# Attention in a hybrid decoder layer: outputs computed transposed with the values as weights, queries and keys stored as high and low parts, and one hand-written order through attention and mix

## The chip, the cores and the metric

The kernel runs on one core of a Trainium2 chip. The metric is the device time of one execution in microseconds (us). The engines are TensorE (PE, with its weight loads PEld), VectorE (DVE), ScalarE (ACT), GpSimd (POOL) and SyncE (SP), which here only issues transfers. ACT and POOL can issue transfers too, each on a queue of its own.

## What is computed

One layer on x of 1024 tokens by 1024 channels, all in float32, with an attention group and a recurrence group side by side:

```python
h = _rms_norm(x, norm_mix_pre)
z = h @ w_in                                  # attention q, k, v (8 heads x 64); RWKV r, k, v, lora
attn = _rms_norm(_dilated_attention(q, k, v), attn_out_gain)
rw = _rwkv7(r, k, v, xw, xa, xg, ...)
x = x + _rms_norm(concatenate([attn, rw]) @ w_out, norm_mix_post)
h = _rms_norm(x, norm_ffn_pre)
f = square(relu(h @ w_ffn_up)) @ w_ffn_down
x = x + _rms_norm(f, norm_ffn_post)
```

The attention has three branches of (window, dilation), (128, 1), (512, 4) and (2048, 16), combined by their softmax denominators. The kernel computes them as one: a strip of additive terms that depend only on the distance of query and key says in how many branches a key counts, and one exponential with the row's extreme as its bias gives numerators and denominators together.

## The kernel before

**Precision.** Most large products are made of three: a float32 matrix is split into a high part in fp32r and the remainder, and `mm3` adds high by high, low by high and high by low. Scores take two: the 128 rows of the weights hold the query's high part (64 channels) over its low part, and the moving matrices hold the key's high (`kh`) or low part (`kl`) twice. The product of exponentials and values is in plain float32, which the trace shows as two records per instruction.

**Stages.** (a) Up to about 446 us come the projections (`z_…`, slabs of 128 output columns, two halves of 512 tokens each) and the recurrence (units `ab`, `e`, `c`, `g`; outputs `O`, `E`, `Y`). The projections are the filling: they run where the recurrence waits. Queries, keys and values of attention (`aq`, `ak`, `av`, one slab per pair of heads) go transposed, as channels by tokens, to DRAM in `zs_d`. (b) Attention, four pairs of heads one after the other. (c) The mix `[A, R] @ W_out` by tiles of 128 tokens, in the order 0, 4, 1, 5, 2, 6, 3, 7, each as an r half (`mxr`) and an a half (`mxa`) that accumulate into `pm`, with a norm and the residual. (d) The feed-forward part, from about 740 us to the end, with products `X`, `Y`, `Z`, `dX`, `dY`, `dZ`; the change leaves it as it is.

**Attention before** is `attn_pair(p)`. SP loads q and k of each head twice, onto partitions 0–63 and 64–127. POOL makes the high parts (`qs` L844, `kh` in `gcopy` L122), DVE the low parts (`qs` L845, `kl` L854). PE transposes the values to `Vt` (keys by channels). For each tile of 128 queries and each head: PE makes scores `pS` in up to two banks, DVE adds the strip and keeps the row's minimum (L890), ACT takes the exponential and its row sum (L893), PE transposes each 128 x 128 block (`pT`, L900), and ACT (L902) or DVE (L904) copies it to `PT`. Then `av` multiplies: `PT` of one block is the weight, 128 columns, and the 64 columns of `Vt` move; a tile of `po` has queries on its partitions. After four query tiles DVE takes reciprocals (L910) and scales (L912), SP stores to `a_d` as tokens by channels (L914), and ACT and DVE sum squares for the norm (L917, L918).

**The entry to the mix.** `half_a` loads a tile of `a_d`, ACT scales it by the norm's factor `sa` (L978), PE transposes it (L964, `mxta`), ACT and DVE split it. So the whole a half waits for `sa`, which needs the last squares. The r halves of three tiles are computed ahead; the third is tied behind the last `po`.

**What sets the order.** The recurrence with its projections is ordered by hand: `drive` walks a list of jobs with their conditions, keeps an estimated time, uses delays from the table `WAIT`, takes a projection step wherever no job is due, and so writes down the order of PE and SP. Attention is not under it: its order comes from the scheduler with a priority (`PRI[3]`), and the projections of the last pair (`rest`) and the weights of the mix are handed to the same scheduler after the first pair. From the first a half on, PE's order is by hand again.

Of the kernel before, what the change touches and what calls it, by code (L numbers as in the profile page):

```python
# [17 lines left out]
P = 128  # L18
# [12 lines left out]
WAIT = {'mrg1.0': 26.0, 'mrg1.3': 4.0, 'mrg2.0': 15.5, 'mrg3.0': 19.5, 'vo3_1': 10.5, 'pre1.0': 9.5, 'e0': 14.5, 'mrg0.0': 29.5, 'vo0_1': 18.5, 'pre3.0': 7.0, 'ab0': 13, 'ab1': 5.0, 'norm3': 3, 'norm2': 3.5, 'vo1_0': 6, 'pre0.0': 6.5, 'vo0_0': 13.0, 'mrg1.2': 5.0, 'vo2_1': 9.5, 'pre2.0': 9.0, 'vo1_1': 6.5, 'vo2_0': 8.0, 'vo3_0': 12.0, 'mrg3.1': 3.5, 'e2': 1, 'c2.2': 1, 'pre1.3': 4, 'T4': 1, 'mrg3.3': 1, 'e4': 1.0, 'VU3': 5.5, 'c3.1': 4.0, 'c6.2': 1.5, 'EO1_1': 1, 'PE4': 5.0, 'e1.0': 2.5, 'e5': 2.5, 'pre2': 0, 'EO0_1': 2, 'e6.0': 0, 'VU7': 1.5, 'ab0.0': 1.5, 'T5': 1, 'e7': 6, 'VU1': 5, 'ab5.0': 4, 'e6': 1.0, 'c4.0': 1, 'EO4_0': 11.0, 'e5.0': 0, 'ab2.0': 2.5, 'c1.1': 2.0, 'e3': 1.5, 'EO5_1': 5, 'VU4': 7.5, 'c1.2': 1, 'ab4': 0, 'e7.0': 2.5, 'EO5_0': 2.5, 'c5.2': 1, 'c2.1': 2.5, 'T1': 5, 'ab3': 0, 'pre1': 0, 'pre2.1': 0, 'mrg2.2': 4, 'c0': 4, 'EO2_1': 3, 'e1': 0}  # L31
# [9 lines left out]
def hybrid_kernel(tc, x, par, cst, strip, win, wup_lora, gup, gnwb, grow, wout, wup, wdown, out, dbg=None):  # L41
# [12 lines left out]
    with (  # L54
# [45 lines left out]
        a_d = dp.tile([S, 512], F32, name="a_d")  # L100
# [6 lines left out]
        bk_d = dp.tile([8, P, 2, 4, P], F32, name="bk_d")  # L107
        v_d = dp.tile([S, 512], F32, name="v_d")
# [228 lines left out]
        def gate():  # L337
            for t in range(8):
# [3 lines left out]
                go = evp.tile([P, 512], F32, name=f"go{t}", tag="ev", bufs=3)  # L342
# [292 lines left out]
        def unit_g(n):  # L635
# [24 lines left out]
            yield 0.0, 11.0  # L660
            nc.sync.dma_start(r_d[ts, :], Y)
            yield 0.0, 0.0

        def v_out(p, hf):
# [8 lines left out]
            vt = evp.tile([P, 512], F32, name=f"vt{p}_{hf}", tag="ev", bufs=3)  # L673
            vc = evp.tile([P, 512], F32, name=f"vc{p}_{hf}", tag="ev", bufs=3)
# [8 lines left out]
        def proj_spill(nm, i, shift):  # L683
            last = [None]

            def ev(hf, pz):
                zt_ = evp.tile([P, 512], F32, name=f"ev_{nm}_{hf}", tag="ev" if i >= 8 else "kr", bufs=3 if i >= 8 else 8)
# [6 lines left out]
                if i < 8:  # L694
                    KR[i, hf] = zt_
                elif i < 12:
                    VZ[i - 8, hf] = zt_
                else:
                    A.dma_start(zs_d[i, :, hf * 512:hf * 512 + 512], zt_)
# [33 lines left out]
        def drive(todo, jobs):  # L733


            now, done, live = 0.0, {}, []
            pre = lambda x: x if isinstance(x, tuple) else (x, 0.0)
            z = slabs(todo, done)
            jobs = list(jobs)
            while jobs or live:  # L740
# [22 lines left out]
                else:  # L763
                    step = next(z, None)
                    if step is None:
# [5 lines left out]
            return z  # L771
# [19 lines left out]
        todo += [(f"{n}{p}", 12 + 4 * j + p, False, "C7" if p == 3 else None) for p in range(4) for j, n in ((0, "aq"), (1, "ak"), (2, "av"))]  # L791
# [25 lines left out]
        order = {j[0]: i for i, j in enumerate(jobs)}  # L817
        with tc.manual_schedule(engines={mybir.EngineType.PE, mybir.EngineType.SP}):
            rest = drive(todo, jobs)
# [3 lines left out]
        ev_ctx = tc.tile_pool(name="ev2", bufs=2)  # L823
        evp = ev_ctx.__enter__()
# [5 lines left out]
        sq4 = cp.tile([P, 4, 8], F32, name="sq4")  # L830
        sa = cp.tile([P, 5, 8], F32, name="sa")[:, 0:2]
        stripT = ap_.tile([P, S], F32, name="stripT", bufs=1)
        nc.sync.dma_start(stripT, strip)

        last_av = [None]

        def attn_pair(p):
            QS, KH, KL = [], [], []
            for h in range(2):
                qr = ap_.tile([P, S], F32, name=f"qr{p}_{h}", tag="raw")  # L840
                for d in range(2):
                    nc.sync.dma_start(qr[own[d]], zs_d[12 + p, h * 64:h * 64 + 64, :])
# [602 lines left out]
```

## Time and profile before

| | |
|---|---|
| median of 3 runs | 1365.77 us (1364.53 to 1368.21) |
| the profiled execution | 1361.23 us, of which the span 1359.4 |
| granted TensorE clock, mean over the span | 0.991 |
| PE busy | 1307.3 us, 96% |
| DVE busy | 914.7 us, 67% |
| ACT busy | 625.0 us, 46% |
| attention, first scores to last output | 469.3 to 637.5 us |
| DMA | 231.02 MB, mean 170 GB/s |

Busy time says when an engine had an instruction in it, not that the engine went at its peak. Matmuls overlap in the pipeline, so the mean length of a record is longer than the distance between the starts of two; it is the distance that sets the time of a group.

### The profile page before, as it was taken

The numbers are of one execution on the slowest core, as the hardware profiler recorded it, in microseconds if no ns is written. First come the engines' busy times: TensorE is split into PE (matmuls) and PEld (weight loads), VectorE is DVE, ScalarE is ACT, GpSimd is POOL, SyncE is SP. The second block draws the span as 40 slices with busy tenths as digits, with TensorE's granted clock in tenths as the row PEclk, the third lists the DMA queues.
The fourth block names the chain that finished last, engine by engine and source line by source line (L and its number), as shares of the span: only waits on it lengthen the run. The fifth ranks groups of instructions, "written<-read, shape, count | busy, mean of one in ns | idle before, by whom it ended". The sixth has DMA issues, their size and how long they took to land.

```text
span 1359.4 us, 22401 instructions
## 1 busy us (share of the span) xinstructions
PE 1307.3 (96%) x8784; PEld 1086.4 (80%) x8784; DVE 914.7 (67%) x1647; ACT 625.0 (46%) x1026; POOL 44.7 (3%) x56
## 2 busy tenths in 40 slices
PE   6999999999999999999998999999999999999997
PEld 5777887788777798988887888888887888888885
DVE  7867658531678567655788986677766786445686
ACT  7652324233555367654656444343434344443442
POOL 0000000000000100110000000000000002000110
PEclk9999999899999999999999999999999999999999
DMA  7346746676685656321434344444366995346564
GB/s 255 114 170 163 194 125 179 184 206 204 182 248 145 194 145 181 102 55 38 138 121 139 132 168 152 168 153 150 132 209 217 322 349 172 95 139 200 186 215 157
DMA packets 161193, 231.02 MB, mean 170 GB/s; under 512 B 51680, under 2 KB 88800, under 8 KB 161088
## 3 DMA queue, kind: packets, MB, share of 16 engines
q1 hardware_dynamic: 153024, 208.62, 48.8%
q10 hardware_dynamic: 8064, 20.98, 4.6%
q8 instruction: 69, 1.13, 0.4%
q14 instruction: 36, 0.29, 0.1%
HBM read 156.66 MB, written 72.89 MB: 169 GB/s over the span
## 4 chain that ended last, share of the span: by engine, by line
PE 77%; DVE 11%; DMA 5%; ACT 4%; issue 2%; SPq 0%; POOL 0%; DVEq 0%; ACTq 0%; POOLq 0%
PE X L47 12%; PE dX L47 9%; PE Z L47 6%; PE pm L47 5%; PE dZ L47 5%; PE po L47 5%; PE dY L47 3%; PE z_av L47 3%; PE z_k L47 3%; PE Y L47 3%; PE pS L47 3%; PE z_v L47 3%; PE z_aq L47 2%; PE pT L900 2%; PE z_r L47 2%
## 5 line engine op out<-in xcount | busy, mean ns | idle before, releaser
L47 PE MATMUL dX<-wow,wou 128*128 128x512 f32 x768 | 176.6, 390 | 3.3 <-ACT wow L1106 1.8
L47 PEld LDWEIGHTS dX<-wow,wou 128*128 128x128 f32 x768 | 143.6, 188 | 35.6 <-DVE wow L1107 3.4
L47 PE MATMUL dZ<-wow,wou 128*128 128x512 f32 x384 | 87.4, 389 | 0.0
L47 PEld LDWEIGHTS dZ<-wow,wou 128*128 128x128 f32 x384 | 72.1, 188 | 14.9
L1106 ACT ACTIVATE wow<-wd 128x1024 fp32r<-128x1024 f32 x40 | 42.3, 1059 | 87.1 <-PE dZ L47 29.8
L1107 DVE TENSOR_TENSOR wou<-ur,wou 128x1024 fp32r<-128x1024 f32 x56 | 72.0, 1288 | 10.8 <-ACT wou L1106 10.5
L47 PEld LDWEIGHTS po<-Vt,PT 128*128 128x128 f32 x576 | 72.6, 191 | 4.8 <-ACT PT L902 2.2
L47 PE MATMUL po<-Vt,PT 128*128 128x64 f32 x576 | 74.0, 269 | 0.7 <-ACT PT L902 0.4
L1107 DVE TENSOR_TENSOR wow<-wd,wow 128x1024 fp32r<-128x1024 f32 x40 | 49.9, 1251 | 36.3 <-ACT wow L1106 35.8
L1106 ACT ACTIVATE wou<-ur 128x1024 fp32r<-128x1024 f32 x56 | 58.6, 1049 | 26.2 <-DMA ur<-u_d 18.8
L893 ACT ACTIVATE S<-S,mn 128x128 f32<-128x128 f32 (+7 forms) x64 | 49.4, 774 | 20.8 <-DVE mn L890 20.7
L890 DVE CUSTOM_DVE_ANT_0 S<-pS,stripT 128x512 f32<-128x512 f32 (+3 forms) x64 | 37.4, 590 | 26.1 <-PE pS L47 15.9
L1193 ACT ACTIVATE r<-u 128x512 f32<-128x512 f32 x48 | 30.1, 627 | 48.4 <-DVE u L1191 48.1
L47 PE MATMUL z_aq<-hT,wh_aq 128*128 128x512 f32 x128 | 47.3, 424 | 3.5 <-DVE ev_v L192 3.5
L47 PE MATMUL pm<-WO,mxr 128*128 128x512 f32 x192 | 48.6, 398 | 0.0
L902 ACT ACTIVATE PT<-pT 128x512 f32<-128x512 f32 (+3 forms) x64 | 32.9, 515 | 32.2 <-PE pT L900 30.2
L1107 DVE TENSOR_TENSOR wow<-TK,wow 128x1024 fp32r<-128x1024 f32 x16 | 20.8, 1301 | 38.9 <-ACT wow L1106 38.9
L47 PE MATMUL Z<-HB,wo 128*128 128x512 f32 x192 | 46.1, 389 | 0.0
L47 PE MATMUL pm<-WO,mxa 128*128 128x512 f32 x192 | 45.8, 394 | 0.0
L900 PE MATMUL pT<-cst,S 128*128 128x128 f32 x288 | 44.4, 276 | 1.0 <-DVE rden L910 0.5
L47 PE MATMUL X<-HB,wo 128*128 128x512 f32 x180 | 43.6, 390 | 1.6 <-ACT HB L1029 1.6
L47 PE MATMUL z_k<-hT,wh_k 128*128 128x512 f32 x128 | 43.2, 398 | 1.7 <-DVE z L223 1.4
(388 smaller groups left out, 3102.5 us busy)
## 6 DMA issues: line engine op xcount, KB each, us to landing
ur<-u_d SPq DMA_DIRECT2D x56, 512.0 KB, 4.2
wd<-in_wdown_dram SPq DMA_DIRECT2D x40, 512.0 KB, 3.9
u_d<-S SPq DMA_DIRECT2D x64, 256.0 KB, 2.1
u_d<-u SPq DMA_DIRECT2D x48, 256.0 KB, 2.1
wr_upa<-in_wup_dram SPq DMA_DIRECT2D x16, 512.0 KB, 3.8
wr_upb<-in_wup_dram SPq DMA_DIRECT2D x16, 512.0 KB, 3.8
TK<-in_wdown_dram SPq DMA_DIRECT2D x16, 512.0 KB, 7.3
x<-in_x_dram SPq DMA_DIRECT2D x8, 512.0 KB, 6.0
```

Of the source, the lines that this page charges most:

```text
L47: return PE.matmul(o, lhsT, rhs, start=start, stop=stop, skip_group_check=True)
L890: V.tensor_tensor_reduce(Sx[:, lo:hi], pS[:, :hi - lo], stripT[:, so:so + hi - lo], 1.0, 3e38 if k == 0 else mn[:, 0:1], OP.add, OP.min, a ...
L893: A.activation(Sx[:, :w], Sx[:, :w], AF.Exp, scale=-1.0, bias=mn[:, nbk - 1:nbk], accum_out=den[:, i, h:h + 1])
L900: PE.transpose(pt[:, j], Sx[:, (4 * k + j) * P:(4 * k + j + 1) * P], ident)
L902: A.activation(PT[:, 0:nb_], pt[:, 0:nb_], AF.Copy)
L1106: A.activation(w[:, 0, 0:n], raw, AF.Copy)
L1107: E.tensor_tensor(w[:, 1, 0:n], raw, w[:, 0, 0:n].bitcast(F32), OP.subtract)
L1193: A.activation(r, src, AF.Relu)
```

## The change

**Projections.** A query or key half is no longer stored as it is. ACT writes the high part (for queries with the scale -0.125), DVE the rest, and both go to `qk_d` by ACT's queue. Attention then loads split parts, six loads per head, and no engine splits there. The last two units of the recurrence store their output by POOL's queue in place of SP's, and the last pair's query projection may start after recurrence unit 5, where it had to wait for unit 7.

**Attention** is cut into jobs for `drive`: `at_load`, `at_vt`, `at_s` (scores of one query tile for both heads, with four `S` tiles in place of three), `at_t` (transposes), `at_r` (reciprocals), `at_v` (outputs of a group of two query tiles). The jobs, the remaining projections (`z_rest`), the loads of `W_out` (`wo_job`) and the r halves of two mix tiles (`r_ahead`) all go into one order of PE and SP; the table `WAIT` gets entries for their delays (not shown).

**Outputs.** In `at_v` the weights are 64 columns of `Vt`, placed on one half of the array's columns for each head, and `PT` moves with 256 columns, the query tiles 2g+1 and 2g side by side (128 where only the odd tile sees the keys). `po` has channels of the two heads on its partitions and queries on its columns. The row sums are per query, so their reciprocals are stored to DRAM (`rd_d`) and read back, spread over 64 partitions per head (`rb`), for the multiplication L964. `a_d` is now channels by tokens. Squares are added over the pairs (`sqa`).

**Mix.** `half_a` loads its tile as it is needed: no transposes and no scaling. Eight matmuls with a matrix of ones sum the squares over channels (`pq`), the norm's factor comes from that, and it is applied to the product: for the first two tiles when the r half is added, for the others by scaling `mr` with its inverse before the product and putting the factor into the following norm. The third r half is no longer ahead.

```diff
             def ev(hf, pz):
...
+                if 12 <= i < 20:
+                    sc = -0.125 if i < 16 else 1.0
...
+                    A.activation(zh, pz, AF.Copy, scale=sc)
+                    V.scalar_tensor_tensor(zl_, pz, sc, zh.bitcast(F32), OP.mult, OP.subtract)
+                    for j, t in enumerate((zh, zl_)):
+                        A.dma_start(qk_d[i - 12, j, :, hs_], t.bitcast(F32))
+                    return
...
-            nc.sync.dma_start(r_d[ts, :], Y)
+            (nc.sync if n < 6 else G).dma_start(r_d[ts, :], Y)
...
+        def at_load(p):
...
+            for h in range(2):
...
+                E = G if p else nc.sync
                 for d in range(2):
+                    E.dma_start(t3[0][own[d]].bitcast(F32), qk_d[p, d, hs_, :])
+                for j in range(2):
+                    for d in range(2):
+                        E.dma_start(t3[1 + j][own[d]].bitcast(F32), qk_d[4 + p, j, hs_, :])
...
+        def at_r(p, g):
...
+            V.reciprocal(rden, at.pop((p, "den", g)))
+            nc.sync.dma_start(rd_d[p, g].rearrange("h s q -> q h s"), rden)
+            yield 0.0, 4.0, None, ((f"V{4 * p + g - 2}", 0.0),) if 4 * p + g > 1 else ()
+            rb = at[p, "rb", g] = ap_.tile([P, 256], F32, name=f"rb{p}_{g}", tag="rb", bufs=2)
+            for h in range(2):
+                nc.sync.dma_start(rb[own[h]], rd_d[p, g, h:h + 1].rearrange("o s q -> o (s q)").to_broadcast([64, 256]))
...
+        def at_v(p, g):
...
+            js = [0, 2 * g + 1] + list(range(1, 2 * g + 1))
+            for x, j in enumerate(js):
+                n = 128 if j > 2 * g else 256
+                for h in range(2):
+                    mm(po[own[h], 0:n], Vt[:, j, h * 64:h * 64 + 64], PTs[h][:, 256 * j:256 * j + n], j == 0, j == 2 * g or g == 0)
...
+            V.tensor_tensor(ao, po, at.pop((p, "rb", g)), OP.mult)
+            if p == 0:
+                A.activation(at["sqa"][:, cols], ao, AF.Square)
+            else:
...
+                V.tensor_tensor(at["sqa"][:, cols], at["sqa"][:, cols], sq, OP.add)
...
+            nc.sync.dma_start(a_d[:, p, cols], ao)
...
+        def half_r(t, tag):
...
+            A.activation(m, m, AF.Copy, scale=sa[:, 2, t:t + 1])
...
-            A.activation(m, m, AF.Copy, scale=sa[:, 1, t:t + 1])
-            return half_t(t, m, "a", tag)
+        def half_a(t):
+            m = mp.tile([P, 4, P], F32, name=f"ma{t}", tag="ma")
+            nc.sync.dma_start(m, a_d[:, :, (t ^ 1) * P:(t ^ 1) * P + P])
+            mx = stg.tile([P, 2, 4, P], F32R, name=f"mxa{t}", tag="wl")
+            A.activation(mx[:, 0], m, AF.Copy)
+            V.tensor_tensor(mx[:, 1], m, mx[:, 0].bitcast(F32), OP.subtract)
+            return mx
...
-                    V.tensor_tensor(src[n], src[n], pm[n], OP.add)
+                    V.scalar_tensor_tensor(src[n], pm[n], sa[:, 1, t:t + 1], src[n], OP.mult, OP.add)
...
+        pq = ps.tile([P, 8, 2], F32, name="pq", tag="a", bufs=1)
+        for t in range(8):
+            mm(pq[:, t ^ 1], at["sqa"][:, t * P:(t + 1) * P], bone)
...
```

Over the program PE's output products go from 288 of 64 moving columns to 128 of 256 and 32 of 128, the 32 transposes of `ma` go, and eight small matmuls come; scores, transposes of `S` and of the values, and the products of the mix keep their numbers.

PE, around the sixth query tile of the first pair, before (each row an instruction with its outputs and inputs and the size, xN for several alike; the first number in a name of `pS`, `pT`, `PT` and `S` is the query tile, the second the head, the third the bank; the last number is a running one):

```order
L47 MATMUL z_av_1_5543<-hT,wh_av_5454 128x512
L900 MATMUL pT_4_1_0_5237<-cst,S_4_1_5225 128x128 x4
L47 MATMUL pS_5_1_0_5270<-kh_1_5054,qs_1_5041 128x512
L47 MATMUL pS_5_1_0_5270<-kl_1_5055,qs_1_5041 128x512
L47 MATMUL po_1_5203<-Vt_5060,PT_4_0_5215 128x64 x5
L47 MATMUL po_1_5203<-Vt_5060,PT_4_1_5236 128x64
L47 MATMUL pS_5_1_1_5274<-kh_1_5054,qs_1_5041 128x256
L47 MATMUL pS_5_1_1_5274<-kl_1_5055,qs_1_5041 128x256
L47 MATMUL po_1_5203<-Vt_5060,PT_4_1_5236 128x64 x4
L47 MATMUL pS_6_0_0_5302<-kh_0_5047,qs_0_5035 128x512
```

And now, around the outputs of the second pair's third group (query tiles 4 and 5; `vt` are the transposes of the values, here for the third pair):

```order
L47 MATMUL pS_6_1_1_5903<-kl_1_5279,qs_1_5277 128x384
L882 MATMUL vt_0_5918<-cst,vT_5874 128x128 x4
L926 MATMUL pT_5_1_0_5924<-cst,S_5_1_5818 128x128 x4
L926 MATMUL pT_5_1_1_5930<-cst,S_5_1_5818 128x128 x2
L882 MATMUL vt_1_5934<-cst,vT_5874 128x128 x4
L47 MATMUL po_2_5940<-PT_2_0_5838,Vt_5510 64x256
L47 MATMUL po_2_5940<-PT_2_1_5839,Vt_5510 64x256
L47 MATMUL po_2_5940<-PT_2_0_5838,Vt_5510 64x128
L47 MATMUL po_2_5940<-PT_2_1_5839,Vt_5510 64x128
...
L47 MATMUL pS_7_0_0_5957<-kh_0_5269,qs_0_5268 128x512
```

Before, the output products of one query tile stand in pieces between scores and transposes, with the projection of the last pair between; now those of two query tiles stand together, the two heads in turn, behind the transposes of the second tile.

DVE, at the same group of the second pair now (`rden` the reciprocals, `rb` what comes back from DRAM, `ao` the scaled output):

```order
L942 RECIPROCAL rden_2_5909<-den_2_5766 128x4
L903 ISA S_6_1_5877,mn_6_1_5879<-pS_6_1_0_5885,stripT 128x512
L903 ISA mn_6_1_5879 128x1
L932 COPY PT_2_0_5838<-pT_5_0_1_5895 128x2x128
L903 ISA S_6_0_5876,mn_6_0_5878<-pS_6_0_1_5899,stripT,mn_6_0_5878 128x384
...
L932 COPY PT_2_1_5839<-pT_5_1_1_5930 128x2x128
L964 TENSOR_TENSOR ao_2_6002<-po_2_5940,rb_2_5965 128x256
L903 ISA S_7_0_5953,mn_7_0_5955<-pS_7_0_0_5957,stripT 128x512
L903 ISA mn_7_0_5955 128x1
```

Before, reciprocal and multiplication (L910, L912) stood on DVE once for four query tiles, one some rows behind the other, both with operands on chip; now they stand once for two, and the multiplication, which needs what comes back from DRAM, is ahead of the next tile's scores.

PE, at the end of attention, before:

```order
L47 MATMUL po_1_6616<-Vt_6473,PT_7_1_6806 128x64 x8
L47 MATMUL pm_0_6944<-WO_5984,mxr_6912 128x512 x3
...
L47 MATMUL pm_1_6945<-WO_6410,mxr_6912 128x512 x3
L964 MATMUL mxta_6999<-cst,ma_6996 128x128 x4
L964 MATMUL mxta_7016<-cst,ma_7013 128x128 x4
L47 MATMUL pm_0_7007<-WO_6423,mxa_7004 128x512 x3
```

and now:

```order
L47 MATMUL po_3_6902<-PT_3_1_6823,Vt_6319 64x256
L47 MATMUL pm_0_6979<-WO_6238,mxa_6976 128x512 x3
L47 MATMUL pm_0_6979<-WO_6385,mxa_6976 128x512 x3
L47 MATMUL pm_0_6979<-WO_6489,mxa_6976 128x512
L47 MATMUL pq<-cst,sqa 128x2 x2
L47 MATMUL pm_0_6979<-WO_6489,mxa_6976 128x512 x2
...
L1082 MATMUL mxtr_7053<-cst,mr_7050 128x128 x4
L47 MATMUL pm_0_6981<-WO_6238,mxa_6987 128x512 x3
```

The first a half now follows the last `po` directly, the norm's sum stands inside it, and the r half that stood between has moved behind.

More of the change, by code (lines that the diff above doesn't have):

```diff
@@ L763, in drive @@
                 else:
-                    step = next(z, None)
-                    if step is None:
+                    step = next(z, "end")
+                    if step == "end" and "z" not in done:
+                        done["z"] = now
+                    elif step in ("end", None):
                         now = min(max([e[0]] + [done[x] + d for x, d in e[4]]) for e in live if all(x in done for x, d in e[4]))
@@ L933, in load_wo, with z_rest @@
                 V.tensor_tensor(w[:, 1], raw, w[:, 0].bitcast(F32), OP.subtract)
[L935 to L945 removed]
+        def z_rest():
+            for step in rest:
+                yield step[0], 0.0
```

339 lines of the change are left out of this document (196 added, 143 removed).

## The prediction

> **What bounds the kernel now.** I read the page's busy times first, then the busy time by stage, then the waits of TensorE, then the groups by line, and the timeline for the rate of single groups. The stages, in the columns stretch, length, busy time of PE, PEld, DVE, ACT and POOL, clock, DMA share:
>
> ```profile
> PE 1307.3 (96%) x8784; PEld 1086.4 (80%) x8784; DVE 914.7 (67%) x1647; ACT 625.0 (46%) x1026; POOL 44.7 (3%) x56
> ```
>
> ```profile
> 469.30:637.50 168.20, 163.88 (x1198) 146.34 (x1198) 104.38 (x270) 101.42 (x223) 15.09 (x14) 1.00 0.40 111
> 637.50:645.50 8.00, 6.51 (x31) 4.96 (x31) 4.29 (x16) 2.67 (x4) 0.00 (x0) 1.00 0.30 78
> 645.50:722.00 76.50, 76.38 (x385) 64.08 (x384) 59.99 (x139) 44.09 (x91) 0.00 (x0) 1.00 0.36 121
> ```
>
> The first stretch is attention (first scores to last output), the second the entry to the mix, the third the mix. The clock is full. A busy PE alone proves little, so its waits in the attention stretch come next (total, times, longest):
>
> ```profile
> PE pS L47 <- DVE kl L854: 1.7, 2, 0.9
> PE pS L47 <- DVE mn L890: 0.5, 1, 0.5
> PE pT L900 <- DVE rden L910: 0.5, 1, 0.5
> PE pS L47 <- POOL kh L122: 0.4, 1, 0.4
> PE po L47 <- ACT PT L902: 0.4, 2, 0.2
> ```
>
> All named waits come to about 4 us of 168, while DVE and ACT are idle for a third of it. TensorE sets the end of this stretch, and what its instructions cost is worth looking at one by one:
>
> ```profile
> L47 PE MATMUL po<-Vt,PT 128*128 128x64 f32 x576 | 74.0, 269 | 0.7 <-ACT PT L902 0.4 <-ACT Vt L864 0.2
> L900 PE MATMUL pT<-cst,S 128*128 128x128 f32 x288 | 44.4, 276 | 1.0 <-DVE rden L910 0.5 <-DVE PT L904 0.3
> L904 DVE COPY PT<-pT 128x128 f32<-128x128 f32 (+3 forms) x32 | 15.7, 490 | 17.9 <-PE pT L900 17.8
> L902 ACT ACTIVATE PT<-pT 128x512 f32<-128x512 f32 (+3 forms) x64 | 32.9, 515 | 32.2 <-PE pT L900 30.2 <-PE pS L47 1.8
> L854 DVE TENSOR_TENSOR kl<-kr,kh 128x1024 fp32r<-128x1024 f32 x8 | 9.8, 1220 | 5.0 <-POOL kh L122 4.9
> L845 DVE SCALAR_TENSOR_TENSOR qs<-qr,qs 64x1024 fp32r<-64x1024 f32 x6 | 7.3, 1222 | 1.5 <-POOL qs L844 1.3
> ```
>
> The 288 f32 products of the values show as 576 records, two passes each. Their mean of 269 ns is latency; the rate is the distance of starts in the timeline (start, length, count last):
>
> ```profile
> 545.09 1.45 PE L47 MATMUL po<-Vt,PT 128*128 128x64 f32 x12
> 546.37 1.04 PE L900 MATMUL pT<-cst,S 128*128 128x128 f32 x8
> 547.25 2.12 PE L47 MATMUL po<-Vt,PT 128*128 128x64 f32 x18
> 549.18 1.18 PE L47 MATMUL pm<-WO,mxr 128*128 128x512 f32 x4
> ```
>
> Twelve po records take 546.37 - 545.09 = 1.28 us and eighteen 1.93: 0.107 us each, no shorter than a transpose's 0.110 with twice the columns, so the 128-column weight load paces them. po fills 576 x 0.107 = 61.6 us, the transposes 288 x 0.110 = 31.7.
>
> **The change, part by part.** (1) *Values as weights.* The 288 matmuls become 128 of 256 columns and 32 of 128, in pairs on two column halves. No such product is in the trace, but two groups use halves:
>
> ```profile
> 403.11 1.15 PE L47 MATMUL O<-VU,TR 128*64 128x64 f32 x32
> 404.19 1.09 PE L47 MATMUL E<-TR,Zp 64*64 64x128 f32 x16
> 405.21 1.16 PE L47 MATMUL p<-AR,K 64*128 64x128 f32 x16
> ```
>
> O has 16 records of 64 columns per half, E 8 of 128: 1024 columns per half either way, in 1.08 and 1.02 us with the way into and out of that shape. Halving the number of records saved 0.06, so 256-column records should take about 0.99. The new po moves (64 x 256 + 16 x 128) x 2 passes = 36,864 columns per half, 36 times 1024: 36 x 0.99 = 36 us. Lower bound: if the 0.2 or so that E's group spends on entry falls away in longer groups, 31; upper: if long records from two halves do not overlap, twice 36 = 72. I take 36, since O is the same weight shape (128*64). **Term: 36 - 61.6 = -25.6.**
>
> The Trainium skill, "TensorE: Matmul & The Clock Gate", Part 3 and "Back-to-back issue gap", has column tiles run concurrently, some 4 ns apart, at N/2.4 + 2.5 ns per matmul. By that, as an estimate, O's 16 pairs would take 0.5 us and the new po about 16, a term of -45. The row of O says 1.08, twice that, so the measurement is kept.
>
> (2) *Outputs arrive transposed.* The 32 mxta transposes go: 32 x 0.110 = 3.5 us on an engine busy 76.38 of 76.5 us. **-3.5.** ACT's scaling of ma goes; six scalings of mr come, same size.
>
> (3) *Entry to the mix.*
>
> ```profile
> 633.77 3.68 PE L47 MATMUL po<-Vt,PT 128*128 128x64 f32 x32
> 637.26 5.71 PE L47 MATMUL pm<-WO,mxr 128*128 128x512 f32 x24
> 637.49 0.69 DVE L912 TENSOR_TENSOR ao<-po,rden 128x512 f32<-128x512 f32 x1 [2.83 <-PE po L47]
> 642.08 0.17 DVE L81 SCALAR_TENSOR_TENSOR sa<-rsm_a,sa 128x8 f32<-128x8 f32 x1
> 642.28 1.47 ACT L978 ACTIVATE ma<-ma,sa 128x512 f32<-128x512 f32 x2 [3.43 <-DVE sa L81]
> 645.54 1.64 PE L47 MATMUL pm<-WO,mxa 128*128 128x512 f32 x6
> ```
>
> Between 637.4 and 645.5 PE does 24 products (0.2275 each, 5.5 us) and eight transposes; 1.8 us are idle. Now the norm's scale is applied after the product, so tile 0 follows the last po at once, and its 5.5 us cover the chain to sa. That chain took 637.5 to 642.25 and grows by a sum, eight small matmuls (0.4) and two tiny operations; with the scaling of mr it ends some 6 us after the last po, so about 1 us of waiting takes the place of 1.8. The 24 products that stood in this gap still have to be done, in the mix; only idle time counts. **-0.8**, between -1.8 and +2. The small matmuls: **+0.4.**
>
> (4) *Queries and keys split at the projections.* This takes 17 us from DVE and all of POOL's splitting out of attention, and with it the 2.1 us that PE waited for kl and kh. In exchange DVE does 16 subtractions of 512 columns beside the projections (0.6 each by L854, 10 us), and ACT issues 16 more DMAs, in a part where PE has spare projections to run; I cost them at 0, and at 3 us if that cover fails. The first scores now wait for 12 loads. In the trace the loads begin 11.5 us after the recurrence's last output and four take 2.4 us to issue:
>
> ```profile
> 445.82 0.34 PE L47 MATMUL O<-VU,TR 128*64 128x64 f32 x6
> 457.56 2.38 SPq L842 DMA_DIRECT2D qr<-zs_d  x4
> qr<-zs_d SPq DMA_DIRECT2D x16, 256.0 KB, 4.8
> ```
>
> 11.5 + 7.1 + 4.8 = 23.4 us, against 96 projection products left to cover it (21.8): 1.6 of waiting, 0 to 4. **-2.1 + 1.6 = -0.5.** The projection of the last pair's queries moves up past the tail of the recurrence; I cost that at 0, within 3 either way.
>
> (5) *Coupling.* The attention stretch shrinks to about 168.2 - 10.9 (48 projection products now ahead of it) - 25.6 - 2 = 130 us. DVE loses 17.1 and gains 16 copies (7.8), two weight splits (2.4) and small reciprocals and sums (3): 100 us, 77% where it was 62%. ACT loses 16 copies (8.2) and gains two splits: 97, 75%. PE's own work was 156 of 168 us: po and transposes 93.3, 96 products of projection and mix 21.8 (0.2275 each), 44 other transposes 4.8, and 192 score products of 73,728 columns in all some 36 (33 at the rate of 512 columns in 0.2275, the rest for short ones). That is a loss of 12 us. Fuller partners in a fixed order cost more; I take 4 us more, from -5 (the order closes gaps) to +16 (the loss more than doubles). **+4.**
>
> **Sum:** -25.6 - 3.5 - 0.8 + 0.4 - 0.5 + 4 = -26.0. The profiled execution took 1361.2 us (span 1359.4 and 1.8 around it), so 1335; the median of the runs, 1365.8, lies 4.5 above it. Forecast: **1339.7, say 1339 us.**
>
> **Rivals.** *DVE and ACT share the bound* (22%). For: each step passes PE, DVE, ACT, PE, ACT or DVE, PE, and ACT waited 50 us on pT and mn already. Against: both keep a quarter of the stretch free. If the loss of 12 us more than doubles, the term is +16 in place of +4: 1351. If it grows by some 28, nothing is left: 1360 to 1364 (4%, no difference).
>
> *The waits shrink* (12%): the loss falls by 5 and po reaches 31: 1326.
>
> *The reciprocals come late* (6%, slower). The denominators are per row, the outputs now transposed; each of the 16 groups sends them to DRAM as 512 single words and reads them back spread over 64 partitions, and DVE holds the multiplication in order ahead of the next scores. Nearest landings, 64-byte runs and a broadcast:
>
> ```profile
> z_d<-Zt SPq DMA_DIRECT2D x2, 128.0 KB, 4.1
> gw<-in_gnwb_dram SPq DMA_DIRECT2D x2, 256.0 KB, 6.0
> r_d<-Y SPq DMA_DIRECT2D x8, 256.0 KB, 3.6
> ```
>
> Slow case 0.2 + 4.1 + 0.6 + 6.0 = 10.9 us. In the order of the second pair's third group, PE has 12 transposes and 4 score products, eight vt transposes and that group's po between, about 6.9 us. 4.0 late, 16 times, is 64; DVE has 30 us free, half of it usable in place: +49 - 26, 1388. It decides from 41 us of lateness, 2.6 per group. Against it: broadcasts of 6 us were taken at a DMA share near 0.7, attention has 0.40, and small stores landed in 2 to 4. The Trainium skill, "DMA: Bandwidth & Descriptors", Specifications, says that runs under 512 B are read, modified and written, which speaks for a slow store of single words; no row here shows one that short.
>
> *The halves do not overlap* (2%, slower): po 72, 1375. Against: O and E.
>
> *The skill's rate holds* (2%): the po term is -45 by that page. In rows: po at half of O's rate, 18 us, so -18 more: 1322.
>
> **How the numbers follow.** The forecast with its own range 1330 to 1346 has 52%. Faster by over 0.3% (4 us, what a measurement here can tell from no change) are forecast, shared bound, shrinking waits and the skill's rate: 88%. Same 4%, slower 8%. The range 1322 to 1360 leaves out the two slower rivals, the far end of the shared bound and half of the smaller times: about 15%.
>
> **What would show it.** po at about 0.11 us per 256-column record with two halves interleaved, 36 us in all; no transposes of ma; the first pm of the attention half within 1 us of the last po; attention near 130 us, PE's named waits under 10. Wrong would be: DVE's multiplication ao waiting for DMA in most groups; PE waiting for ACT's copies of PT or for S throughout; a po rate of twice that.

## The result

The changed kernel takes 1496.35 us (median of 4 runs, 1491.4 to 1503.2) against 1365.15 before: a ratio of 1.096 (95% interval 1.091 to 1.101). 1339 was forecast. The profiled execution took 1503.2 us, its span 1501.4, 142.0 more than before.

Where the 142 us are, by the starts of the first and last instruction of a group in each trace:

| from / to | before | changed | difference |
|---|---|---|---|
| start / last output `O` of the recurrence | 445.9 | 465.5 | +19.6, of which some 10.9 (48 x 0.2275) are the projection products that now stand ahead of it |
| `O` / first score `pS` | 25.6 | 22.1 | -3.5 |
| first `pS` / last `po` | 165.7 | 287.3 | +121.6, though the 48 products are gone from it |
| last `po` / last mix product `mxa` | 89.7 | 92.8 | +3.1 |
| to the end | 632.5 | 633.7 | +1.2 |

The first score before starts at 471.5 us, 2.2 after the 469.3 from which the prediction's table counts the stretch.

It is the attention stretch. Of the page of the changed kernel: the busy time of the engines, the granted clock in 40 slices, and the chain that ended last:

```profile
PE 1326.2 (88%) x8512; PEld 1073.6 (72%) x8512; DVE 914.8 (61%) x1697; ACT 619.6 (41%) x1016; POOL 47.0 (3%) x78
...
PEclk9999999999999677769679999999999999999998
...
PE 61%; DMA 23%; DVE 9%; ACT 3%; issue 2%; SPq 2%; DVEq 0%; ACTq 0%
PE X L47 11%; DMA rd_d<-rden 10%; PE dX L47 8%; PE Z L47 6%; PE pm L47 5%; PE dZ L47 4%; DMA wo<-in_wout_dram 3%; PE dY L47 3%; PE Y L47 3%; PE z_v L47 2%; PE z_aq L47 2%; PE z_ak L47 2%; PE z_r L47 2%; DMA rb<-rd_d 2%; PE z_av L47 2%
```

A group that was not there before, the 16 stores of reciprocals `rd_d`, now makes 10% of the chain. The stretch itself, in the columns of the prediction's first table:

```profile
487.40:775.40 288.00, 166.06 (x902) 121.24 (x900) 95.73 (x292) 96.90 (x214) 18.28 (x36) 0.75 0.47 89
```

TensorE, busy for 97% of this stretch before, is busy for 58% of it, and the clock that it was granted is 0.75 where it was 1.00. The waits in the stretch (total, times, longest), of DVE, of SP and of PE:

```profile
DVE ao L964 <- DMA rb<-rd_d: 92.8, 10, 13.8
DVE WO L985 <- ACT WO L984: 23.9, 3, 10.1
DVE S L903 <- DMA stripT<-in_strip_dram: 23.8, 1, 23.8
DVE ao L964 <- DMA a_d<-ao: 8.4, 1, 8.4
...
SPq L947 <- DMA rd_d<-rden: 126.6, 15, 13.9
...
PE pS L47 <- DVE mn L903: 43.6, 15, 11.3
PE pT L926 <- DVE PT L932: 41.0, 9, 12.3
PE pT L926 <- ACT PT L930: 22.0, 7, 9.4
```

DVE stands for 101 us before 11 of its 16 multiplications by `rb`, SP for 127 us between the store and the loads that read it back. PE waits for work that stands behind the multiplication on DVE: the row minimum of the next scores, the copies of `PT`. How long the transfers take from issue to landing (count, size, median):

```profile
rb<-rd_d SPq DMA_DIRECT2D x32, 64.0 KB, 4.3
rd_d<-rden SPq DMA_DIRECT2D x16, 2.0 KB, 10.2
```

One group in the timeline (start, length, waiting before it):

```profile
605.68 0.17 DVE L942 RECIPROCAL rden<-den 128x4 f32<-128x4 f32 x1
605.88 0.37 SPq L943 DMA_DIRECT2D rd_d<-rden  x1
610.51 2.69 PE L47 MATMUL po<-PT,Vt 128*64 128x256 f32 x24
613.71 0.40 PE L47 MATMUL pS<-kh,qs 128*128 128x512 f32 x1
613.95 0.40 PE L47 MATMUL pS<-kl,qs 128*128 128x512 f32 x1
615.85 1.09 SPq L947 DMA_DIRECT2D rb<-rd_d  x2
620.49 0.42 DVE L964 TENSOR_TENSOR ao<-po,rb 128x256 f32<-128x256 f32 x1 [9.88 <-DMA rb<-rd_d]
621.57 0.80 PE L47 MATMUL pS<-kh,qs 128*128 128x512 f32 x1 [7.23 <-DVE mn L903]
622.16 0.63 PE L47 MATMUL pS<-kl,qs 128*128 128x512 f32 x1
622.59 0.63 PE L47 MATMUL pS<-kh,qs 128*128 128x512 f32 x1
```

The outputs are done at 613.2. From reciprocal to multiplication it is 14.8 us: the store takes 10.0, two loads 4.6. PE has run out of tiles at 614.3 and stands until DVE has multiplied and reduced again. Then it goes at little more than half its speed: the starts of two score products were 0.24 us apart at 613.7 and are 0.43 apart at 622.2.

The forecast of the outputs themselves holds:

```profile
632.42 3.46 PE L47 MATMUL po<-PT,Vt 128*64 128x256 f32 x32
635.81 0.66 PE L926 MATMUL pT<-cst,S 128*128 128x128 f32 x4
```

32 records in 3.39 us are 0.106 each, and 320 of them 34 us (the 64 records of 128 columns counted at the same price), where 36 had been put in.

### The profile page after: what moved, and what is told of

It reads as the page before. It is cut to its first block, busy times and chain, and to the rows that moved or that the text cites. A ratio compares the mean times of both kernels' runs of the same rounds, so it can differ in the third digit from the quotient of the medians.

```text
span 1501.4 us, 22058 instructions
## 1 busy us (share of the span) xinstructions
PE 1326.2 (88%) x8512; PEld 1073.6 (72%) x8512; DVE 914.8 (61%) x1697; ACT 619.6 (41%) x1016; POOL 47.0 (3%) x78
## 4 chain that ended last, share of the span: by engine, by line
PE 61%; DMA 23%; DVE 9%; ACT 3%; issue 2%; SPq 2%; DVEq 0%; ACTq 0%
PE X L47 11%; DMA rd_d<-rden 10%; PE dX L47 8%; PE Z L47 6%; PE pm L47 5%; PE dZ L47 4%; DMA wo<-in_wout_dram 3%; PE dY L47 3%; PE Y L47 3%; PE z_v L47 2%; PE z_aq L47 2%; PE z_ak L47 2%; PE z_r L47 2%; DMA rb<-rd_d 2%; PE z_av L47 2%
## 5 line engine op out<-in xcount | busy, mean ns | idle before, releaser
L926 PE MATMUL pT<-cst,S 128*128 128x128 f32 x288 | 56.6, 339 | 67.8 <-DVE PT L932 41.0
L926 PEld LDWEIGHTS pT<-cst,S 128*128 128x128 f32 x288 | 42.4, 174 | 82.1 <-DVE PT L932 36.9
L47 PE MATMUL pS<-kh,qs 128*128 128x512 f32 (+3 forms) x96 | 46.1, 485 | 47.6 <-DVE mn L903 43.6
L964 DVE TENSOR_TENSOR ao<-po,rb 128x256 f32<-128x256 f32 x16 | 6.8, 424 | 104.5 <-DMA rb<-rd_d 93.3
L47 PEld LDWEIGHTS pS<-kh,qs 128*128 128x128 f32 x96 | 23.0, 240 | 59.2 <-DVE mn L903 50.6
L47 PE MATMUL z_v<-hT,wh_v 128*128 128x512 f32 x128 | 44.0, 410 | 3.7 <-DVE ev_r L194 3.7
```

The source lines that it names most:

```text
L47: return PE.matmul(o, lhsT, rhs, start=start, stop=stop, skip_group_check=True)
L926: PE.transpose(pt[:, j], sx[n][h][:, (4 * k + j) * P:(4 * k + j + 1) * P], ident)
L964: V.tensor_tensor(ao, po, at.pop((p, "rb", g)), OP.mult)
```

## The experiments

Line numbers shift a little from kernel to kernel. The medians are beside the kernel before, which took 1362 to 1365 us in these comparisons; two kernels of different comparisons can therefore be told apart to about 3 us only. Where the text goes by stages, it has them from the profiled runs, cut as in the table above.

### Is it the way of the reciprocals?

Theory A: it is late and holds DVE in order. Rival B: the order by hand and its handovers cost this by themselves. The first kernel, called the kernel without reciprocals below, leaves their store and loads out and multiplies by a constant.

```diff
 def at_r(p, g):
-            nc.sync.dma_start(rd_d[p, g].rearrange("h s q -> q h s"), rden)
...
-            rb = at[p, "rb", g] = ap_.tile([P, 256], F32, name=f"rb{p}_{g}", tag="rb", bufs=2)
-            for h in range(2):
-                nc.sync.dma_start(rb[own[h]], ...)
+            at[p, "rb", g] = at["one"]
```

> This is the changed kernel with the outputs multiplied by a constant tile in place of the reciprocals: the store of the reciprocals to DRAM and the two spread loads of each group are left out, so the attention is not normalized; everything else keeps its place in the planned order. Theory A (the reciprocals' way through DRAM is late and holds DVE in order): DVE's 101 us of waiting before the multiplication go, SP is no longer held 127 us, TensorE's clock stays up; the attention stretch falls from 288 us to about 145, of which some 14 are the first wait for the strip, and the time to 1345 to 1365. Rival B (the order by hand and the handovers between PE, DVE and ACT cost this by themselves, the late reciprocals only stand on top of it): the waits for copies of PT and for the row minimum stay, and the time stays above 1420.

1376.9 us, a ratio of 1.009 [1.007, 1.011]. The way of the reciprocals takes 119.4 us of the 131, and B is out. But the time is 12 us above A's range: the kernel is still slower than before.

Two kernels ask why the store is slow. The same 2 KB in 128 runs of 16 bytes:

```diff
-            nc.sync.dma_start(rd_d[p, g].rearrange("h s q -> q h s"), rden)
+            nc.sync.dma_start(rd_d[p, g].rearrange("h s q -> (h s q)").rearrange("(q f) -> q f", f=4), rden.rearrange("p h s -> p (h s)"))
```

> The store of the reciprocals goes to DRAM in 128 runs of 16 bytes in place of 512 single words, the same 2 KB; the loads are unchanged, so the factors reach the wrong queries and the output is not the reference's. Theory A1 (the store is slow for its number of runs): landing falls from 10.2 us to 3 to 5, the 16 groups get some 5 us each back, 1400 to 1430. Rival A2 (it is slow because it stands behind other transfers on the same engines): landing stays at 9 to 11 and the time within 10 us of the changed kernel's 1496.

1378.7 us in a single run, below the range and within 2 of the kernel without reciprocals. The store in its trace:

```profile
rd_d<-rden SPq DMA_DIRECT2D x16, 2.0 KB, 2.6
```

2.6 us in place of 10.2. So the price is that of 512 single words, not of the place behind other transfers. The number of runs alone is not the price either: the store `z_d<-Zt`, which the prediction took as a bound, writes 2048 runs of 64 bytes and landed in 4.1. Whether the length of the runs decides, or that neighbouring words in DRAM come from different partitions, was not tested. And a complete kernel, in which VectorE transposes the tile in blocks of 32 x 32 before the store:

```diff
+            V.transpose(rt, r32)
+            for b in range(4):
+                nc.sync.dma_start(rd_d[p, g, :, b], rt[32 * b:32 * b + 4])
```

> The complete computation with the changed kernel's order and its way of the reciprocals through DRAM, but VectorE first transposes the 128 x 4 tile in 32 x 32 blocks, so that the store has 16 runs of 128 bytes (four small transfers) in place of 512 single words. Theory A1 (the 512 single words are the price): landing at 2 to 4 us as with the 16-byte runs, 1375 to 1390 with 16 transposes on VectorE and three more transfers per group on SP. Against it, if only the 16-byte form with its factors for the wrong queries were fast for another reason: above 1450.

1390.0 us (1.020 [1.017, 1.023]): 106 us come back with the same way through DRAM, the same two loads per group and the same order. From first `pS` to last `po` it takes 173.7 us, the kernel without reciprocals 174.4; of the 13 us between the two, 10 lie in the feed-forward part, which is taken up in the last section. SP's wait for the store:

```profile
SPq L953 <- DMA rd_d<-rt: 21.2, 12, 7.2
```

21 us where it was 127. Could the plan have hidden the slow store? Only the two assumed durations were changed:

```diff
-            yield 0.0, 4.0, None, ((f"V{4 * p + g - 2}", 0.0),) ...
+            yield 0.0, 10.5, None, ((f"V{4 * p + g - 2}", 0.0),) ...
-            ... WAIT.get(f"rb{4 * p + g}", 3.5)
+            ... WAIT.get(f"rb{4 * p + g}", 6.0)
```

> Only two numbers of the plan that sets the order are changed: the store is assumed to take 10.5 us in place of 4.0 and the spread loads 6.0 in place of 3.5, about what the trace of the changed kernel shows; the instructions are the same. If the damage is only that the multiplication stands too early in DVE's order, other work now stands in front of it and the time falls below 1440. If the way of about 17 us cannot be covered because the two output banks hold only two groups of some 8 us each, DVE's wait for the loads becomes a wait of others for the banks and the time stays within 1470 to 1500.

1482.9 us in a single run, 13 less than the median of the changed kernel and 9 less than its fastest run. The order was wrong about the store, but right durations in the plan don't cover it: DVE still waits 71 us for `rb`. That two groups in flight leave too little else to do is the likely reason; more groups in flight were not tried.

### Reciprocals on chip

A transpose by TensorE, then two matmuls with a selection matrix of four rows that spread each row over 64 partitions:

```diff
+            PE.transpose(po[0:4, 256:384], rden.rearrange("p h s -> p (h s)"), ident)
+            A.activation(rT, po[0:4, 256:384], AF.Copy)
+            for s in range(2):
+                mm(po[:, 256 + 128 * s:384 + 128 * s], at["sel"][:, s], rT)
+            A.activation(rb, po[:, 256:512], AF.Copy)
```

> The reciprocals stay on chip: the 128x4 tile is transposed by TensorE, copied by ACT, spread over 2 x 64 partitions by two matmuls with a four-row selection matrix into the unused half of the outputs' bank, and copied by ACT. Theory A: as without the reciprocals, plus some 0.4 us of PE and 0.6 us of ACT for each of 16 groups: 1350 to 1375, with a latency from reciprocal to factor of about 2 us in place of 18. Rival B: above 1430.

1394.7 us. Its outputs are not those of the reference (the likely reason is that its factors share a bank with outputs that are still being accumulated); it is taken here for the time of its work alone. With a bank of their own and a shorter chain (the row sums transposed behind the last transposes, the reciprocal taken by DVE from the result):

```diff
+            PE.transpose(zt[0:4, 256:384], at.pop((p, "den", g)).rearrange("p h s -> p (h s)"), ident)
+            V.reciprocal(rT, zt[0:4, 256:384])
+            yield 0.06, 0.9
+            for s in range(2):
+                mm(zt[:, 128 * s:128 * s + 128], at["sel"][:, s], rT)
```

> Reciprocals on chip by another order: the row sums themselves are transposed behind the last transposes of S, into a bank that no output accumulates in, DVE takes the reciprocal of the 4 x 128 tile, two matmuls spread it, ACT copies it. If the 1394.7 us of the first on-chip version came from its hops (DVE, PE, ACT, PE, ACT standing in order between the scores), the shorter chain gives 1375 to 1387; if any on-chip way costs PE, DVE and ACT its own work in a stretch where all three are near their limit, it stays at 1390 to 1400. The 16-byte runs gave 1378.7.

1409.8 us: worse, and above both ranges. Of the 12 us between the two profiled runs 7 are in the attention stretch and 4 in the feed-forward part. Its waits in attention:

```profile
PE pT L930 <- ACT PT L934: 19.0, 15, 8.9
PE pS L47 <- DVE mn L907: 7.4, 10, 3.6
PE pS L47 <- DMA kl<-qk_d: 7.0, 1, 7.0
PE rz L47 <- DVE rT L949: 6.4, 9, 1.2
```

The spreading matmul stands in PE's order and waits 6.4 us for DVE (`rz`), where the transfers had been waited for by nobody but the multiplication. PE also waits 19.0 us for ACT's copies of `PT`, 11.0 with the runs of 128 bytes; ACT now copies the factors too, but whether that is the reason was not tested.

### The rest: 38 us between the kernel without reciprocals and the forecast

Theory E: the entry. In the kernel without reciprocals, the first stretch of attention and PE's waits:

```profile
484.00:498.00 14.00, 1.25 (x6) 0.73 (x4) 0.00 (x0) 0.60 (x1) 6.10 (x12) 0.66 1.04 268
```

```profile
PE pT L928 <- ACT PT L932: 13.3, 11, 8.6
PE pS L47 <- DVE mn L905: 8.2, 10, 3.6
PE pS L47 <- DMA kl<-qk_d: 6.1, 1, 6.1
PE pS L47 <- DMA kh<-qk_d: 3.8, 1, 3.8
PE pm L47 <- DVE mxr L1021: 3.6, 2, 2.1
```

PE works 1.25 of 14 us, while the DMA engines are full (share 1.04, 268 GB/s) with the first pair's 12 loads, the strip, and the second pair's 12. One longer wait, 8.6 us for ACT's copies, is a later burst: ACT had a split of `W_out` in front of them, and its load came late. First the strip was moved ahead, and the second pair's loads later in the plan:

```diff
+                if p == 0 and h == 0:
+                    nc.sync.dma_start(at["strip"], strip)
...
-["left"] if p == 1 else [f"S{n - 9}"]
+["left", "S3"] if p == 1 else [f"S{n - 9}"]
```

> The 16-byte runs (factors to the wrong queries) with two edits at the entry to attention: the strip is loaded after the first head's queries and keys, not after all twelve loads, and the second pair's twelve loads start after the fourth query tile, not at once. Theory E (about 13 us at the entry are lost because strip and second pair share the DMA engines, whose share is 1.04 from 482 to 500): 1363 to 1370. Rival (the first scores are late anyway, or the loads collide later): above 1375.

> On-chip reciprocals by the shorter chain with the two edits at the entry: 10 to 14 us below the version without them, so 1362 to 1375, which would still not be faster than the kernel before; below 1360 only if the entry also held later work.

1380.2 and 1412.1 us: nothing gained on either base. The timeline shows why:

```profile
481.41 1.04 POOL L863 DMA_DIRECT2D qs<-qk_d  x2 [13.35 <-PE pS L47]
...
484.39 1.09 SPq L866 DMA_DIRECT2D kl<-qk_d  x2
...
495.62 0.45 PE L47 MATMUL pS<-kl,qs 128*128 128x128 f32 x1 [8.76 <-DMA kl<-qk_d]
```

The later place in the plan held little back: GpSimd waits for PE's first scores only, not for the fourth tile, and issues these loads from 481.4 on, ahead of the first pair's last keys at 484.4, which land 11 us after their issue. So the loads were put into SP's written order, and the splits of `W_out` behind their loads:

```diff
-                E = G if p else nc.sync
+                E = nc.sync
...
 def load_wo(k, pool, tag):
             nc.sync.dma_start(raw, wout[k * P:(k + 1) * P, :])
+            yield 0.0, 9.0
```

> The kernel with the constant factor (reciprocals left out, the attention is not normalized), and its transfers paced: the loads of the later pairs go by SP in its planned order, the second pair's behind the first group's store, in place of GpSimd's queue where nothing held them back; the strip is loaded behind the first head; and ACT's and DVE's splits of W_out are placed 9 us of plan time behind their loads. Theory D (what is left of the loss without the reciprocals, 1376.9 us, are bursts of split queries and keys that delay the second head's keys at the entry by about 12 us and a load of W_out, with ACT's copies queued behind it, by about 9): 1350 to 1360. Rival (the three engines' handovers in a fixed order set the stretch, and the waits only move): above 1370.

> The same pacing with the reciprocals on chip, by the shorter chain with 2.5 us of plan time between the reciprocal and the spreading matmuls; complete computation. By theory D 1375 to 1385 (the first on-chip versions, 1394.7 and 1409.8, less 15 to 25); by the rival 1400 or more.

> The same with the paced transfers (later pairs' loads by SP in the planned order, the strip behind the first head, the splits of W_out 9 us of plan time behind their loads) and with the second pair's values loaded ahead of its queries and keys, since in the paced kernel without reciprocals TensorE waited 6 us for them. Theory D: 1360 to 1372. If pacing only moves the waits once SP also carries the reciprocals: 1375 or more.

1369.2 us without reciprocals, 7.7 less; 1399.8 with them on chip, 10 less than the chain unpaced (its spreading stands 1.6 us later in the plan, too); but 1399.4 (median of three runs) with the way through DRAM, 9.4 more than unpaced. In that last kernel:

```profile
PE vt L886 <- DMA vT<-zs_d: 21.3, 2, 13.8
```

SP now carried reciprocals and loads, and the values came late. Pacing moves a part of the wait.

Leaving loads out prices them. All pairs on the first pair's queries and keys, then all heads on the first head's:

```diff
 def at_load(p):
+            if p:
+                at[p] = at[0]
+                yield 0.0, 0.0
+                return
             for h in range(2):
+                if h:                              # second kernel only
+                    at[p].append(at[p][0])
+                    continue
```

> The kernel with the constant factor, and the later three pairs work on the first pair's queries and keys: the reciprocals and 36 of the 48 loads of split queries and keys (9 MB) are left out, everything else stands as in the changed order. If the bursts of these loads hold the entry, W_out and ACT's copies behind it: 1355 to 1363 in place of 1376.9. If the handovers of a fixed order do: 1372 or more.

> As before it, and all heads work on the first head's queries and keys: six loads in all are left (reciprocals and 42 of 48 loads left out). If the wait at the entry is the time of its 12 loads on full DMA engines, it shrinks by some 6 us: 1349 to 1357. What is then left above the forecast of 1339 is neither reciprocals nor loads. If the entry waits for something else: within 2 us of the run with one pair.

1363.2 and 1358.4 us, against 1376.9 with all loads: 13.7 us for the later bursts (11 by the ratios to the kernel before), 4.8 more for half of the entry's. 18.5 of the 38 us are loads. 19.4 are left, although neither a reciprocal nor more than six loads of queries and keys is there. (In both kernels some products of the first a half also moved ahead of the last outputs in PE's order; from the last pair's third group to the first `X` the first of them takes 99.7 us, the kernel with all loads 99.2, so nothing was gained by that.)

Does the written order cause them? The jobs in the same sequence, PE and SP left to the scheduler:

```diff
-        drive(jobs, rest, {})
         pe_order.__exit__(None, None, None)
+        drive(jobs, rest, {})
```

> The 128-byte runs with attention's jobs emitted in the same sequence, but PE and SP not held to it: the scheduler orders them by its own costs and priorities, as in the kernel before. If the written order of PE and SP is what keeps the stretch from the forecast 130 us: below 1365. If the stretch is held by what the engines hand over and load, whatever the order: 1375 to 1400.

1411.2 us against 1390.0: the scheduler is worse at it. Giving the written order up does not bring the loss back; that another written order would is not excluded.

### Undoing the split storage

Queries and keys stored as they are, eight loads per pair, GpSimd and DVE split them in attention as before; reciprocals in 128-byte runs:

```diff
-                if 12 <= i < 20:
+                if False:
...
+                G.tensor_scalar(t3[0], qr, -0.125, 0.0, op0=OP.mult, op1=OP.add)
+                V.scalar_tensor_tensor(t3[0][64:128], qr[64:128], -0.125, t3[0][64:128].bitcast(F32), OP.mult, OP.subtract)
+                gcopy(t3[1], kr)
+                V.tensor_tensor(t3[2], kr, t3[1].bitcast(F32), OP.subtract)
```

> Complete computation, reciprocals in 128-byte runs, and the fourth part of the change undone: queries and keys go to DRAM as they are, eight loads per pair in place of twelve, GpSimd and VectorE split them in attention as in the kernel before. If the split storage costs more by its loads than it saves on VectorE: 1375 to 1385 against 1390.0. If VectorE's 17 us in attention weigh more: 1395 or more.

1395.5 us, but by a wait of the experiment's own making:

```profile
PE z_ak L47 <- ACT wh_ak L131: 22.8, 1, 22.8
```

The raw tiles took places of the ring through which the last projections' weights come. With the first pair's raw tiles in the ring of the score tiles, complete, and without reciprocals:

```diff
-stg.tile([P, S], F32, name=f"{nm}{p}_{h}", tag="wr", bufs=3)
+stg.tile(...) if p else pl.tile([P, S], F32, name=f"{nm}{p}_{h}", tag="S", bufs=4)
```

> As the complete kernel with unsplit queries and keys, but the first pair's raw tiles lie in the ring of the score tiles, not in the one that also takes the weights of the last projections: in the kernel before this one PE waited 22.8 us for those weights. If the split storage is a net loss, now that this wait is gone: 1368 to 1378, against 1390.0 with split storage. If VectorE's 17 us in attention weigh as much as the loads: 1385 to 1395.

> Unsplit queries and keys and the constant factor (reciprocals left out): what the outputs on halves, the written order and the mix are worth without the two costs found so far. The forecast's own terms for these parts, with the 19 us that the run with one head's loads left open, give 1358; below 1350 would say that the open part came with the split storage too; above 1368 that VectorE's work in attention is now on the path.

1374.3 us (1.008 [1.006, 1.011]) and 1364.1 (1.001 [0.999, 1.002]): 15.6 and 12.8 less than with split storage (11 in place of 12.8 by the ratios). Split storage is a loss of that size. The complete one is the best version found that keeps the new outputs, and it doesn't beat the kernel before; of the 18 us between their profiled runs, 11 lie in the feed-forward part (last section).

What holds the version without reciprocals and with unsplit loads; its attention stretch, and PE's waits in it:

```profile
477.90:641.80 163.90, 134.72 (x901) 99.32 (x899) 113.67 (x308) 97.47 (x216) 27.40 (x37) 0.96 0.40 120
```

```profile
PE pS L47 <- DVE mn L910: 6.8, 11, 1.3
PE pT L933 <- DVE PT L939: 5.1, 6, 1.7
PE pS L47 <- POOL kh L124: 5.0, 1, 5.0
PE pT L933 <- ACT PT L937: 4.8, 9, 1.0
PE pm L47 <- DVE mxr L1026: 3.4, 2, 1.9
PE pT L933 <- ACT S L915: 2.3, 2, 1.7
```

But for one of 5.0 us no wait is large any more: 33, most under 1 us, and 29 us in all where the kernel before had 4. DVE is busy for 69% and ACT for 59%. PE's work for the outputs became shorter by 28 us (61.6 - 34) and its named waits longer by 25.

## Why the prediction was wrong

**The bound** was read rightly: before, PE set the end of attention, at 0.107 us per record of `po`. That the weight load paced these records is argued; no run separates it.

**Values as weights: right.** 36 us were forecast, 0.106 x 320 = 34 measured; the rows of `O` and `E` carried over to longer records. The rival with half of O's rate, 18 us, did not come. By "TensorE: Matmul & The Clock Gate" of the Trainium skill (Part 3 and Back-to-back issue gap) the estimate was about 16 us; the trace has 34, and the measurement decides. Whether each record takes 0.21 and two overlap, or 0.106 alone, no run tells, since no f32 product of 256 columns without a partner is in a trace.

**No transposes of `ma`, entry to the mix: right.** Together -3.9 us were put in. In the kernel with 16-byte runs the time from the last `po` to the last mix product went from 89.7 to 85.9, and the first a half started 0.3 us after the last `po`. In the changed kernel the late reciprocals delay it by 3.5 us, and the stretch is 92.8.

**The failed step is the wait for the reciprocals.** The sum has no term for it. It stood among the rivals, with its place, its mechanism and the in-order multiplication, at 6% and 1388 us. It was mis-sized: the store was bounded by "nearest landings" of 64-byte runs, 4.1 us, and took 10.2 at the median (8.7 to 16.0). With it the way was 14.8 us in the group shown in place of 10.9 at worst; PE had work for 8.7 us of it, where 6.9 had been put in. It also missed two things that follow: SP stands between store and loads (127 us) with the loads of `W_out` behind it, and after a long wait PE comes back slower (0.43 us per score product for 0.24). The evidence against it ("small stores landed in 2 to 4") was of stores of 128 KB and more, in runs of 64 bytes and more. "DMA: Bandwidth & Descriptors" of the Trainium skill, Specifications, which was cited there (runs under 512 B are read, modified and written), spoke for a slow store and was outweighed; but the 16-byte runs, under 512 B too, landed in 2.6 us, so that line alone doesn't tell the two apart. Shown: 106 us in a complete kernel, 118 with the 16-byte runs, 119 without the way through DRAM.

**Queries and keys split at the projections: wrong, -0.5 for +11 to +16 us.** The step "11.5 + 7.1 + 4.8" counted the issue and the landing of single loads. 12 loads of 256 KB for the first pair, 12 for the second and the strip take about 25 us at 268 GB/s (an estimate from their sizes), and the second pair's begin 11 us after the first pair's; leaving out 42 of 48 loads gave 18.5 us. The relief of DVE that was to pay for it was worth less than the loads: with DVE's 17 us of splitting back in the stretch and eight loads per pair for twelve, the time fell.

**Coupling: +4 where some 20 stand.** The rival "DVE and ACT share the bound" had the mechanism, with 1351 and 1362 for two sizes; with reciprocals and most loads left out the time was 1358.4, 19 us above the forecast, and with unsplit loads 1364.1. In the first of them it is 155.7 us from first `pS` to last `po`, where about 130 were forecast. That single waits of about 1 us add up to this is read from the waits and was not separated by a run of its own. Some 5 us of it may be the recurrence: in the kernel with one head loaded its last output starts at 462.1 us, where 445.9 + 10.9 = 456.8 was forecast (458.5 to 465.5 in the others with the same work ahead of it).

So of the 157 us between forecast and median: 106 to 120 the store of single words, 11 to 18 the split loads, about 20 the coupling; the ranges overlap, because each was taken away with others in place, and the coupling is what is left over, not a cause shown by a run.

## What to carry to other kernels

A small transfer is not priced by its bytes: here 2 KB in 512 single words took 10.2 us to land, in 128 runs of 16 bytes 2.6, and 128 KB in runs of 64 bytes 4.1; a 32 x 32 transpose on VectorE ahead of the store took its cost out of the attention stretch. When a result changes its axis, everything that is still indexed by the old one has to cross too; that crossing, not the matmul that gave the reason for the change, is to be bounded, and a row with the same run length has to be found or the bound left open. Where an engine that is the bound gets faster by a sixth, its partners' handovers have to be counted one by one: here PE's named waits grew by about as much as the matmuls gave.

## What the runs showed that had not been expected

The price of the store (512 words 10.2 us, 128 runs of 16 bytes 2.6) is above. Two more:

TensorE after a wait. The starts of two score products of 512 columns were 0.24 us apart before a wait of 7.2 us and 0.43 after it; over the whole stretch the granted clock was 0.75, where it was 1.00 before, so a long wait cost more than itself.

The feed-forward part, which no edit touches, was slower in some kernels. From the first `X<-HB` to the last `dX` it took 619 to 622 us before, in the changed kernel (also with the other durations in the plan), and in all those without reciprocals or with factors for the wrong queries, 625 in the first on-chip version, but 628 to 632 in the eight complete ones of attention under 200 us (both later on-chip kernels and their paced forms, the 128-byte runs and what was built on them). In steady stretches, with unsplit loads, complete (first) and without reciprocals (second):

```profile
1138.00:1238.00 100.00, 100.00 (x430) 80.42 (x429) 50.97 (x43) 43.19 (x52) 6.96 (x4) 1.00 0.41 126
```

```profile
1130.00:1230.00 100.00, 100.00 (x443) 82.84 (x442) 52.74 (x44) 42.49 (x51) 6.96 (x4) 1.00 0.40 125
```

430 matmuls in 100 us against 443, at a granted clock of 1.00 in both, and PE never idle. The cause is open; it means that some 9 us of the complete versions' 1374 and 1390 are not attention's, and that complete and incomplete kernels are better compared by the attention stretch than by the whole time.
